# Order of the value products, pace of the feed and bank of the v products in a streaming Conformer step

## The chip, the cores and the metric

The kernel runs on one core of a Trainium2 chip. The metric is device time in microseconds (us). TensorE (PE) multiplies, with weights loaded beside it (PEld); VectorE (DVE), ScalarE (ACT) and GpSimd (POOL) do the elementwise work; SyncE (SP) issues the DMAs. Matrix products are summed in PSUM, which has eight banks.

## The reference, cut to what matters

Two layers, for a prompt of 4096 rows and a sample of 64 rows with a cache of 128 rows; the model has 1024 columns, 16 heads of 64 in two groups of 8, one K/V head for each group.

```python
# layer 0: gated convolution module -> x
kv = rmsnorm(x, kv_g) @ w_kv                     # shared K and V, 2 heads of 64 each
# layer 1
z = rmsnorm(x, pre_g) @ w_in                     # q and gate, 1024 columns each
q, gate = split(z, 2)
s = q / 8 @ k.T - slope * |q_pos - k_pos|        # a query chunk of 64 sees 3 chunks of keys:
                                                 # two past ones and its own
m = max(s.max(), sink); p = exp(s - m)
o = (p / (p.sum() + exp(sink - m))) @ v          # the value products
y = (o * silu(gate)) @ w_out
x = x + rmsnorm(y, post_g)
```

Outputs are y for both streams, the convolution state and the K/V rows of the last window.

## The kernel before, in words

Each f32 operand is split into a high and a low float16 half, and a product is three matmuls: high by high, high by low, low by high. Layer 0 takes the first 1540 us or so. Then come two stages that the change touches.

**Projections (`proj_qkv`, from about 1560 to 1965 us).** Blocks of 256 rows, sixteen of the prompt and one of the sample. The q product of a block is Strassen's scheme of seven products (`strassen`, L942), with accumulators X and W in the PSUM banks tagged "mm" (three) and Z in those tagged "cv" (two, `ps_cz`). X is added to over four products, with a copy by ACT (P1, U2, U3; L953, in the trace U_q and P_q) between them. The order of jobs is written out: p1, p5, K, p6, p2, p7, V of rows 0 to 127, p4, V of rows 128 to 255, p3; after each job comes one step that prepares the next block (`prep_x1`): norms and transposes through PSUM tiles tagged "tr" (two banks; L1023, L1040, L1044). `v_job` (L1161) sums in a tile psv that is also tagged "tr"; `put_v` reads it with ACT (L1140) and DVE (L1141) and stores it.

**Attention (from about 2006 us to the end).** A unit is 128 queries (i) of a block (b) by one K/V head (kv): four units a block, 66 in all, of which 62 are whole (those of the first rows and of the sample are shorter). A unit goes through:

- `att_scores`: scores in "cv" banks (sc, L1491 and L1492), bias and maximum on DVE (L1495), then `stats`: exponentials on ACT (L1522);
- `att_probs`: scaling on POOL (L1541); transposes on PE (ptr, L1557) of three kinds of 128 keys, 0 (two chunks of the past), 1 (one chunk of the past and one of the present) and 2 (the present ones), each put into a float16 tile pT, high half by ACT (L1565, L1562) and then low half by DVE (L1566, L1563);
- `att_values` (L1570): 20 matmuls (pv, L1591) into one bank tagged "s2", of 128 rows by 64 columns each, in pairs for the two heads of a pair (`s_`). For the first 64 queries (par 0) five pairs: kind 0 by high and low V, kind 1 by V; for the second 64 (par 1) five pairs: kind 2, then kind 1;
- `att_out`: times the gate on DVE (L1604), high half by ACT (L1607), low half by DVE.

Between these steps stands filling work from a queue `fill`: the gate projection of the next block (`gate_jobs`, Strassen again: sx_g, sw_g, sz_g, L935), seven products valued 2.75, and the output products of finished rows (`y_jobs`: psy, L179, L180, L182), two halves valued 5.2 for each 128 rows. `filler` takes jobs while a balance is above zero; each unit adds `per` to it in six shares. `force` issues what is left of a block's gate products when its first unit begins. For the last two blocks `per` is worked out from what is left.

The framework then schedules: it goes through this order with a model of the engines' times, and on each engine places the first instruction in program order among those whose inputs are ready by the model. So the order on an engine isn't the program's, and a tile's buffers are given out among those free. It adds all semaphores. DMAs are issued on SP.

Of the kernel before, what the change touches and what calls it, by code (L numbers as in the profile page):

```python
# [12 lines left out]
F32 = mybir.dt.float32  # L13
# [5 lines left out]
P = 128  # L19
# [36 lines left out]
TAIL_D = 0.5  # L56
TAIL_P = 5.2
EARLY_P = 10.0
PER = 10.0
SHARE = (0.2, 0.1, 0.2, 0.1, 0.2, 0.2)  # L60
G_AT = 2

# [5 lines left out]
def tile_streaming_conformer(  # L68
# [17 lines left out]
    pst = ctx.enter_context(tc.tile_pool(name="ps", bufs=2, space=PSUM))  # L86
# [4 lines left out]
    def ps_cv(shape, name):  # L91
        return pst.tile(shape, F32, tag="cv", name=name, bufs=2)

    def ps_s2(shape, name):
        return pst.tile(shape, F32, tag="s2", name=name, bufs=1)
# [79 lines left out]
    def mm3(out, wts, mov, low_last=False):  # L175
        n = len(wts)
        if low_last:
            for i in range(n):
                nc.tensor.matmul(out, wts[i][0], mov[i][0], start=i == 0, stop=False)  # L179
                nc.tensor.matmul(out, wts[i][0], mov[i][1], start=False, stop=False)  # L180
            for i in range(n):
                nc.tensor.matmul(out, wts[i][1], mov[i][0], start=False, stop=i == n - 1)  # L182
            return
        for i in range(n):
            wh, wl = wts[i]
            mh, ml = mov[i]
            nc.tensor.matmul(out, wh, mh, start=i == 0, stop=False)  # L187
            nc.tensor.matmul(out, wh, ml, start=False, stop=False)  # L188
            nc.tensor.matmul(out, wl, mh, start=False, stop=i == n - 1)  # L189
# [27 lines left out]
    def big(shape, dt, name):  # L217
        return wk.tile(shape, dt, tag="big", name=name, bufs=6)
# [207 lines left out]
    with ExitStack() as ph:  # L426
# [64 lines left out]
        ps = pst.tile([P, 4, P], F32, tag="tr", name="pst_apg")  # L491
# [264 lines left out]
        for b in range(SB):  # L756
# [9 lines left out]
            if b + 1 == SAMP_AT:  # L766
                hTs, l, nm, tr = in_jobs(SB)
# [357 lines left out]
    def proj_qkv(b, ht, pool):  # L1125
        t0, T, _, _, _, samp = bb[b]
# [11 lines left out]
        def put_v(src, n, scale, dst, name):  # L1138
            o = pool.tile([P, 2, P], F16, tag="vo", name=name)
            nc.scalar.activation(o[:n, 0], src, AF.Copy, scale=scale)  # L1140
            nc.vector.scalar_tensor_tensor(  # L1141
                out=o[:n, 1], in0=src, scalar=scale, in1=o[:n, 0], op0=ALU.mult, op1=ALU.subtract
            )
            nc.sync.dma_start(out=dst, in_=o[:n])
# [16 lines left out]
        def v_job(i):  # L1161
            n = min(P, T - i * P)
            last = samp or t0 + i * P + n == SEQ
            ps = pst.tile([P, 2 * P], F32, tag="tr", name=f"psv_{b}_{i}")
            wts = [(hT[0][:, kb, i * P : i * P + n], hT[1][:, kb, i * P : i * P + n]) for kb in range(KB)]
            lo = 0 if last else P
            mv = [(w_kv.at(0, kb, lo, 2 * P - lo), w_kv.at(1, kb, lo, 2 * P - lo)) for kb in range(KB)]
            mm3(ps[:n, lo : 2 * P], wts, mv)
            put_v(ps[:n, P:], n, SX / SP, v_scs[WIN:] if samp else v_scr[t0 + i * P : t0 + i * P + n], f"vo_{b}_{i}")
            if last:  # L1170
                kv = big([P, D], F32, f"kvo_{b}")
                nc.scalar.activation(kv[:n, : 2 * P], ps[:n], AF.Copy, scale=1.0 / SP)
                for c, dst in ((0, ck_s if samp else ck_p), (P, cvv_s if samp else cvv_p)):
                    nc.sync.dma_start(
                        out=dst[0, WIN - n : WIN].rearrange("t k d -> t (k d)"), in_=kv[:n, c : c + P]
                    )
# [21 lines left out]
        if samp:  # L1198

            def q_half(half):  # L1200
                ps = ps_mm([P, KH, CH], f"psqs_{half}")
                samp_half(wq, hT, tT, half, ps)
                put_q(half, 0, ps)

            return [k_job, lambda: v_job(0), lambda: q_half(0), lambda: q_half(1)]
# [7 lines left out]

        q = strassen(wq, hT, tT, tmp, out, f"q{b}")
        return [q[0], q[1], k_job, q[2], q[3], q[4], lambda: v_job(0), q[5], lambda: v_job(1), q[6]]

    hts = {}
# [74 lines left out]
    def gate_jobs(b):  # L1292
        t0, T, _, _, _, samp = bb[b]
        gts = CT.setdefault(b, {})["gts"] = {}
        h, t = HT[b]

        def put(nh, i, src, n):
            if i not in gts:
                gts[i] = quad([P, 2, KH, P], F32, f"gt_{b}_{i}")
            go = gts[i][:, nh, :, :n]  # L1300
            nc.scalar.activation(go, src, AF.Tanh, scale=0.5 / SP)
            nc.vector.scalar_tensor_tensor(out=go, in0=go, scalar=1.0, in1=src, op0=ALU.add, op1=ALU.mult)

        if samp:

            def g_half(half):
                ps = ps_mm([P, KH, CH], f"psgs_{half}")
                samp_half(wg, h, t, half, ps)
                put(half, 0, ps, CH)

            return [(2.8, lambda: g_half(0)), (2.8, lambda: g_half(1))]

        def out(nh, th, ps, add):
            src = ps
            if add is not None:
                src = add if (nh, th) == (1, 1) else ps
                nc.vector.tensor_tensor(out=src, in0=ps, in1=add, op=ALU.add)
            put(nh, th, src, P)

        jobs = [(2.75, fn) for fn in strassen(wg, h, t, tmp, out, f"g{b}")]  # L1320
        if b + 1 < nb:
            jobs.append((0.0, lambda: gate_load(b + 1)))
        return jobs
# [134 lines left out]
    with ExitStack() as ph:  # L1458
# [111 lines left out]
        def att_values(b, i, kv):  # L1570
            u = U[b, i, kv]
            npar, first, samp, nm, pts = (u[z] for z in ("npar", "first", "samp", "nm", "pts"))
            prev = vt.get((b, i - 1)) if (i > 0 or samp) else vt.get((b - 1, 1))
            cur = vt[(b, i)]
            po = ps_s2([P, 4, P], f"pv_{nm}")
            vs = slice(kv * HD, kv * HD + HD)
            for par in range(npar):
                mms = []
                full = (0, prev) if par == 0 else (2, cur)
                if full[0] in pts:  # L1580
                    pT, v = pts[full[0]], full[1]
                    for ph_, vh in ((0, 0), (1, 0), (0, 1)):
                        mms.append((v[:, 0, vh, vs], pT[:, ph_]))
                if par == 0 or not first:
                    v = cur if par == 0 else prev
                    for vh in range(2):
                        mms.append((v[:, 1 + par, vh, vs], pts[1][:, par]))
                for q_, (w, m) in enumerate(mms):
                    for s_ in range(2):
                        sl = slice(s_ * 64, s_ * 64 + 64)  # L1590
                        nc.tensor.matmul(po[sl, :, par * CH : par * CH + CH], w, m[:, :, sl], start=q_ == 0, stop=q_ == len(mms) - 1)  # L1591
            u["po"] = po
# [96 lines left out]
        for k, (b, i, kv) in enumerate(units):  # L1689
# [3 lines left out]
            if ui == 0 and b + 1 < nb:  # L1693
                load_att(b + 1)
                fill.extend((c, (b + 1, "g"), fn) for c, fn in gate_jobs(b + 1))
            per = PER
            if b >= nb - 2:
# [17 lines left out]
            while sc:  # L1715
                sc.popleft()()
            att_values(b, i, kv)
            if stats is not None:
                stats()
# [46 lines left out]
```

## Time and profile before

| | us |
|---|---|
| median of 3 runs (2954.96 to 2958.47) | 2955.04 |
| the profiled execution, in all | 2958.04 |
| its span | 2956.3 |
| PE busy | 2803.8 (95%) |
| PEld busy | 1788.6 (61%) |
| DVE busy | 2322.2 (79%) |
| ACT busy | 1885.9 (64%) |
| POOL busy | 1833.2 (62%) |

Shares are means over stages with different limits: up to about 1300 us DVE and POOL are busy nine tenths of the time beside PE, afterwards PE stands alone. A row of PE's instructions in order of time has the start, the time from the first start to the last end, the line, and how many like instructions follow one another; matmuls overlap, so starts tell more than lengths. In brackets stands how long the engine was idle before, and what ended it.

### The profile page before, as it was taken

The numbers are of one execution on the slowest core, as the hardware profiler recorded it, in microseconds if no ns is written. First come the engines' busy times: TensorE is split into PE (matmuls) and PEld (weight loads), VectorE is DVE, ScalarE is ACT, GpSimd is POOL, SyncE is SP. The second block draws the span as 40 slices with busy tenths as digits, with TensorE's granted clock in tenths as the row PEclk, the third lists the DMA queues.
The fourth block names the chain that finished last, engine by engine and source line by source line (L and its number), as shares of the span: only waits on it lengthen the run. The fifth ranks groups of instructions, "written<-read, shape, count | busy, mean of one in ns | idle before, by whom it ended". The sixth has DMA issues, their size and how long they took to land. (4 is left out here: it accounts for less than half of the span.)

```text
span 2956.3 us, 63971 instructions
## 1 busy us (share of the span) xinstructions
PE 2803.8 (95%) x24441; PEld 1788.6 (61%) x24441; DVE 2322.2 (79%) x4373; ACT 1885.9 (64%) x4405; POOL 1833.2 (62%) x1967
## 2 busy tenths in 40 slices
PE   8989999999999988989998999998999999999998
PEld 5444444444444443444458999996777777767774
DVE  6999899999999999988885777745666666656665
ACT  6787776877777675556665777635555555555554
POOL 8899899998898999977742344323333333333332
PEclk9999999999999999999999999999999999999999
DMA  5311211211100125566656666673234223323321
GB/s 183 111 46 41 74 51 43 65 51 47 47 36 33 51 81 169 162 195 196 189 165 192 212 217 229 209 241 118 91 105 125 93 94 122 106 93 98 115 73 48
DMA packets 260601, 341.30 MB, mean 115 GB/s; under 512 B 40549, under 2 KB 184677, under 8 KB 259525
## 3 DMA queue, kind: packets, MB, share of 16 engines
q1 hardware_dynamic: 260293, 337.20, 35.7%
q8 instruction: 192, 3.15, 0.5%
q14 instruction: 116, 0.95, 0.1%
HBM read 206.46 MB, written 130.72 MB: 114 GB/s over the span
## 5 line engine op out<-in xcount | busy, mean ns | idle before, releaser
L597 POOL TENSOR_TENSOR pacc<-pacc,pr 128x512 f32<-128x512 f32 x704 | 908.2, 1306 | 65.6 <-ACT pr L588 38.5
L611 DVE SCALAR_TENSOR_TENSOR acc<-u,pt,acc 128x512 f32<-128x512 f32 x1088 | 789.3, 750 | 17.8
L588 ACT ACTIVATE pr<-u,pt 128x512 f32<-128x512 f32 x704 | 485.6, 716 | 164.2 <-POOL pacc L597 152.2
L1522 ACT ACTIVATE p<-p,st 128x192 f32<-128x192 f32 (+1 forms) x520 | 227.9, 440 | 76.6 <-DVE st L1516 76.3
L1495 DVE CUSTOM_DVE_ANT_0 p<-sc,bias 128x192 f32<-128x192 f32 (+1 forms) x520 | 160.4, 349 | 90.3 <-PE sc L1492 76.0
L1541 POOL TENSOR_TENSOR p<-p,st 128x768 f32<-128x768 f32 (+2 forms) x130 | 186.6, 1456 | 40.9 <-DVE st L1537 26.9
L187 PE MATMUL ps_a<-hT,w_a 128*128 128x512 f16 (+1 forms) x528 | 197.3, 374 | 6.9 <-ACT sg L680 5.4
L187 PE MATMUL ps_gl<-hT,w_gl 128*128 128x512 f16 (+1 forms) x528 | 198.7, 376 | 3.5 <-ACT sig L751 1.9
L188 PE MATMUL ps_gl<-hT,w_gl 128*128 128x512 f16 (+1 forms) x528 | 198.4, 376 | 0.9 <-DVE hT L206 0.9
L187 PE MATMUL ps_gt<-hT,w_gt 128*128 128x512 f16 x512 | 195.8, 382 | 2.8 <-ACT sig L751 2.8
L189 PE MATMUL ps_gl<-hT,w_gl 128*128 128x512 f16 (+1 forms) x528 | 198.4, 376 | 0.0
L179 PE MATMUL psy<-w_oa,hl 128*128 128x512 f16 x512 | 197.3, 386 | 1.0 <-DVE c L611 1.0
L179 PE MATMUL psy<-w_ob,ogT 128*128 128x512 f16 x512 | 194.9, 381 | 3.1 <-ACT ogT L1607 3.1
L180 PE MATMUL psy<-w_oa,hl 128*128 128x512 f16 x512 | 197.5, 386 | 0.0
L188 PE MATMUL ps_a<-hT,w_a 128*128 128x512 f16 (+1 forms) x528 | 197.4, 374 | 0.0
L189 PE MATMUL ps_a<-hT,w_a 128*128 128x512 f16 (+1 forms) x528 | 197.3, 374 | 0.0
L189 PE MATMUL ps_gt<-hT,w_gt 128*128 128x512 f16 x512 | 195.7, 382 | 0.0
L188 PE MATMUL ps_gt<-hT,w_gt 128*128 128x512 f16 x512 | 195.7, 382 | 0.0
L180 PE MATMUL psy<-w_ob,ogT 128*128 128x512 f16 x512 | 195.0, 381 | 0.0
L935 PEld LDWEIGHTS <-w_gS 128*128 128x128 f16 x3072 | 178.4, 98 | 22.7 <-issue 17.6
L935 PEld LDWEIGHTS <-w_qS 128*128 128x128 f16 x3072 | 178.6, 99 | 3.2 <-issue 2.6
L1371 POOL COPY qs<-qraw 128x512 f16<-128x512 f16 (+1 forms) x132 | 75.1, 614 | 136.7 <-PE sc L1492 76.5
(360 smaller groups left out, 7045.7 us busy)
## 6 DMA issues: line engine op xcount, KB each, us to landing
x<-in_x_prompt SPq DMA_DIRECT2D x32, 512.0 KB, 3.7
g_scr<-sg SPq DMA_DIRECT2D x64, 256.0 KB, 2.4
c_scr<-c SPq DMA_DIRECT2D x64, 256.0 KB, 2.0
c<-c_scr SPq DMA_DIRECT2D x32, 512.0 KB, 4.7
g<-g_scr SPq DMA_DIRECT2D x32, 512.0 KB, 4.8
x<-x_scr SPq DMA_DIRECT2D x128, 128.0 KB, 3.6
h_scr<-hTb SPq DMA_DIRECT2D x32, 512.0 KB, 3.7
h_scr<-tTb SPq DMA_DIRECT2D x32, 512.0 KB, 3.6
```

The lines of the kernel that those rows point to most:

```text
L179: nc.tensor.matmul(out, wts[i][0], mov[i][0], start=i == 0, stop=False)
L180: nc.tensor.matmul(out, wts[i][0], mov[i][1], start=False, stop=False)
L187: nc.tensor.matmul(out, wh, mh, start=i == 0, stop=False)
L188: nc.tensor.matmul(out, wh, ml, start=False, stop=False)
L189: nc.tensor.matmul(out, wl, mh, start=False, stop=i == n - 1)
L588: nc.scalar.activation(dst[:, :T], u[:, k : k + T], AF.Identity, scale=wdw[:, j, k : k + 1], bias=pt[:, j, R_DWB : R_DWB + 1] if k == 0 el ...
L597: nc.gpsimd.tensor_tensor(out=pacc[:, :T], in0=pacc[:, :T], in1=dst[:, :T], op=ALU.add)
L611: nc.vector.scalar_tensor_tensor(out=dst[:, :T], in0=u[:, k : k + T], scalar=wdw[:, j, k : k + 1], in1=src[:, :T], op0=ALU.mult, op1=ALU.add,)
L935: nc.tensor.matmul(ps[:, j, :], w[:, wz, kb, j * P : j * P + P], rhs(rz, kb), start=first and j + kb + wz + rz == 0, stop=last and j == KH ...
L1495: nc.vector.tensor_tensor_reduce(out=pbuf[:, t, par * 192 + lo : par * 192 + 192], in0=ps[:, tt, :nk], in1=bias[:, lo:], scale=1.0, scalar ...
L1522: nc.scalar.activation(pp, pp, AF.Exp, scale=2.0 ** -(kv * 4 + t) / SQ, bias=st[:, 1, par, t : t + 1], accum_out=st[:, 3, par, t : t + 1],)
L1541: nc.gpsimd.tensor_tensor(out=pp, in0=pp, in1=st[:, 4, par, :, None].to_broadcast([P, 4, 3 * CH - lo]), op=ALU.mult)
```

## The change

In three places. `att_values` goes through the two halves of the queries the other way round, par 1 first, and for the two full kinds takes the low half of pT before the high half. PER, what a unit adds to the balance of the filling queue, goes from 10.0 to 9.7. And psv, the sum of the v products, is taken from the "cv" banks, where Z and later the scores are, instead of the "tr" banks.

```diff
-PER = 10.0
+PER = 9.7
...
         def v_job(i):
             n = min(P, T - i * P)
             last = samp or t0 + i * P + n == SEQ
-            ps = pst.tile([P, 2 * P], F32, tag="tr", name=f"psv_{b}_{i}")
+            ps = ps_cv([P, 2 * P], f"psv_{b}_{i}")
...
             po = ps_s2([P, 4, P], f"pv_{nm}")
             vs = slice(kv * HD, kv * HD + HD)
-            for par in range(npar):
+            for par in reversed(range(npar)):
                 mms = []
                 full = (0, prev) if par == 0 else (2, cur)
                 if full[0] in pts:
                     pT, v = pts[full[0]], full[1]
-                    for ph_, vh in ((0, 0), (1, 0), (0, 1)):
+                    for ph_, vh in ((1, 0), (0, 0), (0, 1)):
                         mms.append((v[:, 0, vh, vs], pT[:, ph_]))
```

## The prediction

> **What bounds the kernel now.** I read the page first, then the table of stages, then TensorE's instructions in order of time, then the table of waits. The span is 2956.3 us, and the profiled execution took 2958.04 us in all, 3.0 us above the median of the three runs (2955.04 us). The sum below is made against the 2958.04 us and then moved down by those 3.0 us.
>
> ```profile
> span 2956.3 us, 63971 instructions
> ...
> 1700.00:1950.00 250.00, 239.32 (x4070) 233.87 (x4068) 174.85 (x352) 174.99 (x492) 90.79 (x78) 1.00 0.64 210
> 2100.00:2300.00 200.00, 198.21 (x2103) 143.47 (x2101) 125.89 (x389) 112.09 (x367) 72.01 (x120) 1.00 0.35 111
> ...
> 2364.00:2422.00 58.00, 57.80 (x625) 42.22 (x623) 37.03 (x114) 32.51 (x103) 20.46 (x34) 1.00 0.33 106
> 2644.20:2703.50 59.30, 57.86 (x624) 42.26 (x624) 36.97 (x114) 32.14 (x104) 20.50 (x34) 1.00 0.33 104
> ```
>
> The table of stages has busy us of PE, weight loads, DVE, ACT and POOL, then granted clock, DMA share and GB/s. The change touches two stages: the projections (some 1560 to 1965 us) and attention (2006 us to the end). In attention PE is busy 198.21 of 200 us; DVE, the next engine, has 125.89. So PE's own work sets the pace there, and what is taken from it is taken from the time. The last two rows are one attention block each (four units of 128 queries by one KV head): the early kind takes 58.0 us, the late kind 59.3, with the same busy time.
>
> Busy time doesn't tell whether PE streams or stumbles; the start times do. One unit, on PE, in order of time:
>
> ```profile
> 2403.61 0.89 PE L935 MATMUL sx_g<-hl,w_gA 128*128 128x128 f16 x13
> 2404.43 0.30 PE L1591 MATMUL pv<-pT,v_(6, 0)_29279 128*64 128x256 f16 x2
> 2404.66 0.56 PE L935 MATMUL sx_g<-hl,w_gA 128*128 128x128 f16 x7
> ...
> 2405.60 0.41 PE L1591 MATMUL pv<-pT,v_(6, 0)_29279 128*64 128x256 f16 x4
> ...
> 2406.77 0.41 PE L1591 MATMUL pv<-pT,v_(6, 1)_29285 128*64 128x256 f16 x4
> ...
> 2408.66 0.30 PE L1591 MATMUL pv<-pT,v_(6, 1)_29285 128*64 128x256 f16 x2
> ...
> 2409.33 0.41 PE L1591 MATMUL pv<-pT,v_(6, 1)_29285 128*64 128x256 f16 x4
> 2409.57 0.39 PE L1591 MATMUL pv<-pT,v_(6, 0)_29279 128*64 128x256 f16 x4
> 2409.89 0.26 PE L1491 MATMUL sc<-ks,qs 128*128 128x192 f16 x1
> ...
> 2411.13 2.06 PE L935 MATMUL sx_g<-tl,w_gS 128*128 128x128 f16 x34
> 2413.03 0.38 PE L179 MATMUL psy<-w_ob,ogT 128*128 128x512 f16 x1
> ```
>
> The order is not the program's: each part of the value products (pv) is put in as soon as its input is ready, between gate products of other work (sx_g). The 20 pv matmuls of this unit stand in five runs (2, 4, 4, 2, 8).
>
> **What a run costs.** The 34 sx_g take 2413.03 - 2411.13 = 1.90 us, 56 ns each. The 13 before the first run should then end at 2403.61 + 0.73 = 2404.34; pv starts at 2404.43: 0.09 us to get in. Another unit has all its 20 in one run:
>
> ```profile
> 2079.33 1.22 PE L935 MATMUL sx_g<-tl,w_gS 128*128 128x128 f16 x19
> 2080.48 0.52 PE L1591 MATMUL pv<-pT,v_(0, 1)_23834 128*64 128x256 f16 x6
> 2080.83 0.71 PE L1591 MATMUL pv<-pT,v_(1, 0)_24763 128*64 128x256 f16 x10
> 2081.38 0.39 PE L1591 MATMUL pv<-pT,v_(0, 1)_23834 128*64 128x256 f16 x4
> 2081.70 1.51 PE L935 MATMUL sw_g<-hl,w_gA 128*128 128x128 f16 x24
> ```
>
> Two halves of 64 columns run side by side, so 20 matmuls are ten pairs; from 2080.83 to 2081.38 are five pairs, 0.11 us each. Ten take 1.10 of the 1.22 us from 2080.48 to 2081.70: 0.12 us to get out. A run so costs 0.09 + 0.12 = 0.21 us, however long it is. It is paid where the matmuls' shape changes between 128*64 and 128*128.
>
> Over attention I count 203 runs off the same view, from the first to the last:
>
> ```profile
> 2006.32 0.74 PE L1591 MATMUL pv<-pT,v_(0, 0)_23828 128*64 128x256 f16 x10
> ...
> 2943.76 0.38 PE L1591 MATMUL pv<-pT,v_(16, 0)_38519 128*64 128x256 f16 x2
> ```
>
> 195 of them are in the 62 units with 20 matmuls; in these, cuts stand before the 3rd matmul 22 times, the 7th 15, the 11th 37, the 13th 51 and the 17th 8. That is 203 x 0.21 = 43 us of changing over, on the engine that sets the pace.
>
> **Part 1: the order of the value products.** The change adds and removes no instruction here. It puts the second 64 queries (par 1) first, and in them the low half of the last transposed part. That half is the last thing DVE makes for the unit:
>
> ```profile
> 2407.76 0.69 DVE L1566 TENSOR_TENSOR pT<-ptr,pT 128x512 f16<-128x512 f32 x1
> ...
> 2410.66 0.70 DVE L1604 SCALAR_TENSOR_TENSOR pv<-pv,gt 128x512 f32<-128x512 f32 x1
> ```
>
> It ends at 2408.45; its first reader now is the first pair of the unit's last run, at 2409.33, 0.9 us later. If the rest of the products may not overtake, all 20 are ready at once and go as one run. Whether they may not: both par halves write one PSUM bank, in different columns. A case of two outputs in one bank is in the scores:
>
> ```profile
> 2383.05 0.25 PE L1492 MATMUL sc<-ks,qs 128*128 128x192 f16 x1
> ...
> 2383.65 0.25 PE L1492 MATMUL sc<-ks,qs 128*128 128x192 f16 x1
> ...
> 2383.94 0.36 DVE L1495 CUSTOM_DVE_ANT_0 p<-sc,bias 128x192 f32<-128x192 f32 x1 [2.10 <-PE sc L1492]
> ```
>
> DVE had been idle 2.10 us, and its first output was done at 2383.30; still it starts at 2383.94, when the other output of the bank (2383.65 + 0.25 = 2383.90) is done. Work on one bank is kept in program order even where columns differ. I take it that par 0 can't overtake par 1.
>
> Runs after: one per unit, and cuts by other work with precedence. Before, once everything was ready (13th to 20th matmul), such a cut came in 8 units of 62; for 20 instead of 8 matmuls 2.5 times as many, 20. So 62 + 20 = 82 runs instead of 195: 113 x 0.21 = **23.7 us less**. The bounds: 62 runs, 133 x 0.21 = 27.9 less; and below, rival 1.
>
> What covers the later start: the unit's output (L1604) waits for the last product. The one run would start at 2409.33 or sooner and end 1.2 us later, at 2410.5, against 2409.89 before, 0.6 us later; here L1604 starts only at 2410.66 and loses nothing. Elsewhere DVE already waits for pv:
>
> ```profile
> DVE pv L1604 <- PE pv L1591: 40.8, 38, 4.7
> ...
> PE pv L1591 <- ACT pT L1565: 2.7, 4, 1.7
> ```
>
> (us in total, times, longest.) DVE has 37% idle, so a longer wait there costs it nothing; behind it are ACT's copy and the output product, for which PE has other work queued. PE itself has waited 2.7 us for pT in all attention. Cost taken: 0; the end on the other side is rival 3.
>
> **Part 2: PER 10 to 9.7.** No instruction is added; the place of filling work (gate and output products) in program order moves. A block supplies 7 x 2.75 + 4 x 5.2 = 40.05; four units took 40.0 and now take 38.8. Working the queue's arithmetic through, the fill left after a unit falls to 5.2 in early blocks now and to 10.4 in late ones; it would stay at 10.4 or more from the second block on and at 15.6 or more from the sixth, and three gate products (8.3 in all) would be issued by force at starts of late blocks. Loads of the next block's gate inputs on SP follow the last gate product and so move later by up to one unit, behind which 10.4 of output products still stand; SP issues as many as before. The trace prices this by its two kinds of block: idle 0.20 us of 58.0 and 1.44 of 59.3. If every early block became the late kind, 7 x 1.24 = 8.7 us more; if all six late ones became the early kind, 7.4 us less. The new pattern is neither, so I take 0, with both ends kept.
>
> **Part 3: psv into the bank pair of Z and scores.** Z is the second Strassen accumulator (sz_q). In the projections the v product waited for DVE's transposes to give back a "tr" bank:
>
> ```profile
> PE psv L187 <- DVE x L1044: 14.3, 8, 8.9
> ...
> 1563.37 0.58 DVE L1337 TENSOR_SCALAR nsk<-sk 128x1 f32<-128x1 f32 x8 [11.38 <-DMA sk<-in_b_sinks]
> 1564.70 0.29 PE L187 MATMUL psv<-w_kv,hTb 128*128 128x128 f16 x1 [8.87 <-DVE x L1044]
> 1565.20 0.58 ACT L953 COPY U_q<-sx_q 128x512 f32<-128x512 f32 x1
> ...
> 1775.29 0.23 PE L187 MATMUL psv<-w_kv,hTb 128*128 128x128 f16 x1 [0.87 <-DVE x L1044]
> 1777.05 0.58 ACT L953 COPY U_q<-sx_q 128x512 f32<-128x512 f32 x1
> 1777.68 0.72 PE L935 MATMUL sx_q<-tTb,w_qA 128*128 128x128 f16 x10 [0.37 <-ACT U_q L953]
> 1780.36 0.22 PE L187 MATMUL psv<-w_kv,hTb 128*128 128x128 f16 x1
> 1781.50 0.28 DVE L1141 SCALAR_TENSOR_TENSOR vo<-psv,vo 128x128 f16<-128x128 f32 x1
> ```
>
> That wait of 14.3 us goes. What is late next: the product behind v waits for ACT's U copy, which isn't moved. At 1777.68 v would be done 0.87 us sooner and sx_q would still start at 1777.68. The one long wait (8.87 us) comes from DVE standing behind a load of the sinks; U is copied only at 1565.20, so PE waits on. Gain taken 0; at most the 14.3. The cost: Z holds one of the two "cv" banks, so a block's second v product needs the first one's bank, free at 1781.78; it started at 1780.36. That is 1.42 us late, unless PE does Z's last 48 products (2.7 us at 56 ns) first, which nothing here holds back. Cost taken 0, at most rival 2.
>
> **Sum.** 2958.0 - 23.7 + 0 + 0 = 2934.3; less 3.0 for the median: **2931 us**, 0.8% faster.
>
> **Rivals.**
> 1. Par 0 overtakes (columns apart count as free). Then the cuts before the 3rd and the 13th matmul go (low and high halves wait together), those before the 7th, 11th and 17th stay, and the 11th becomes as frequent as the 13th was, 51: 62 + 15 + 51 + 16 = 144 runs, 51 x 0.21 = 10.7 less: 2944 us. For it: scores show DVE against PE, not PE against PE. Chance 0.15.
> 2. The "cv" banks stall PE in the projections: the second v product waits 1.42 us per block, its own bank comes free as much later (1787.5 instead of 1786.1), and the next block's Z, due about 1786.6, waits 0.9: 2.3 x 15 blocks = 35 us, so 2931 + 35 = 2966 us, slower. It decides from 24 / 15 = 1.6 us per block. Against it: Z's last products can go first. PE is busy 239.32 of 250 there, so there is little slack to hide it in. Chance 0.07.
> 3. The saved changes turn into waits: 0.6 us later output in 62 units is 37 us; if two thirds of it came through because PE is short of other work, the 24 us are gone: 2955. Against: PE idles 1.79 of 200 us. Chance 0.08. The Trainium skill, Perfetto Trace Analysis, "Identifying the Most-Contended Engine", speaks for this rival: it says that matmul busy time is no good measure of headroom and that weight-load busy time is. By that rule the stage is at 143.47 of 200 us, 72%, and nothing need be gained. The start times of the trace (56 ns, row after row) disagree, and I go by them.
> 4. The feed also heals the late blocks: 7.4 less, 2924 us. Chance 0.12.
>
> My own case has 0.58. Faster by over 0.2% (5.9 us, about what a measurement of this kernel can tell from no change): 0.58 + 0.15 + 0.12 = 0.85; within 0.2%: 0.08; slower: 0.07. The range: below, 27.9 and 7.4 less, and some of the 14.3 that I took as nothing, 2917; above, rival 1 with part of the feed's 8.7, 2950. Outside lie rivals 2 and 3.
>
> **What would show it.** Right: pv on PE in runs of 20, 70 to 100 runs in all, blocks of 56 to 58 us, and PE busy time in attention lower with as little idle time. psv's wait for DVE gone from the table of waits and sx_q's wait for U_q larger by about as much. Wrong: runs of 6 and 10 (rival 1); PE's psv or sz_q waiting for vo L1141 (rival 2); psy waiting for ogT or pv for pT far above 2.7 us (rival 3); blocks at 59 us and idle sx_g waits (the feed).

## The result and the profile after

The changed kernel takes 2937.04 us (median of 6 runs, 2935.51 to 2940.13), the kernel before, beside it, 2955.0 us: a ratio of 0.9941 [0.9928, 0.9954]. So it is 18 us, 0.6%, faster. The profiled execution took 2936.48 us in all.

The page of the changed kernel first, then its table by stretches (busy us of PE, weight loads, DVE, ACT and POOL, with the number of instructions, then clock, DMA share and GB/s):

```profile
span 2934.5 us, 63935 instructions
...
PE 2774.2 (95%) x24441; PEld 1795.8 (61%) x24441; DVE 2336.9 (80%) x4373; ACT 1883.6 (64%) x4405; POOL 1844.1 (63%) x1967
```

```profile
1700.00:1950.00 250.00, 234.38 (x3928) 230.02 (x3928) 174.84 (x346) 171.25 (x487) 88.29 (x76) 0.99 0.63 206
2100.00:2300.00 200.00, 196.22 (x2171) 149.58 (x2170) 136.40 (x407) 113.00 (x365) 74.53 (x124) 1.00 0.37 116
2100.00:2850.00 750.00, 740.17 (x8247) 565.00 (x8247) 504.12 (x1510) 429.60 (x1384) 280.04 (x454) 1.00 0.34 106
```

The last row has this counterpart in the kernel before:

```profile
2100.00:2850.00 750.00, 738.41 (x7964) 539.98 (x7962) 474.85 (x1444) 411.59 (x1322) 262.05 (x437) 1.00 0.33 104
```

PE's share is 95% in both. The counts are what differs: in the same 750 us of attention PE does 8247 matmuls where it did 7964, and DVE, ACT and POOL do more too. Each of the larger kinds of matmul grew by 3 to 5%, so it is not a shift to shorter ones. In the projections (1700 to 1950 us) it is the other way: 3928 matmuls instead of 4070, with 15.6 us of idle time instead of 10.7. The change gained in one stage and lost in the other.

Unit 27, whose 20 value products stood in five runs, on PE in order of time:

```profile
2401.36 0.38 PE L179 MATMUL psy<-w_ob,ogT 128*128 128x512 f16 x1
2401.67 0.52 PE L1591 MATMUL pv<-pT,v_(6, 1)_29285 128*64 128x256 f16 x6
2402.03 0.71 PE L1591 MATMUL pv<-pT,v_(6, 0)_29279 128*64 128x256 f16 x10
2402.57 0.39 PE L1591 MATMUL pv<-pT,v_(6, 1)_29285 128*64 128x256 f16 x4
2402.89 0.26 PE L1491 MATMUL sc<-ks,qs 128*128 128x192 f16 x1
```

They are one run now. The first six read the V rows of the unit's own block, as par 1 does. The run still costs what was read off before: 2402.89 - 2401.67 = 1.22 us for ten pairs of 0.11 us.

The waits, first of attention and then of the projections (us in total, times, longest):

```profile
DVE pv L1604 <- PE pv L1591: 44.0, 32, 6.3
...
PEld L1591 <- issue: 9.9, 34, 1.0
...
PE ptr L1557 <- DVE pT L1566: 7.6, 3, 3.8
...
PE psy L179 <- ACT ogT L1607: 3.5, 3, 2.4
PE ptr L1557 <- POOL p L1541: 3.1, 3, 2.1
...
PE pv L1591 <- DVE pT L1566: 1.2, 2, 1.0
```

```profile
PE psv L187 <- DVE vo L1141: 17.1, 13, 2.6
PE sx_q L935 <- ACT U_q L953: 10.3, 3, 9.5
```

In attention the waits have changed places. The transposes wait for DVE's pT, which frees their bank, where before they waited for POOL:

```profile
PE ptr L1557 <- POOL p L1541: 8.8, 12, 2.2
...
PE ptr L1557 <- DVE pT L1566: 0.3, 1, 0.3
```

In all, PE's idle time from the first value product to the end is much the same: 31.0 of 918.4 us after, 31.8 of 950.0 before. In the projections the wait for DVE's transposes (14.3 us) is gone, and one of 17.1 us for vo stands in its place. One such place:

```profile
1777.99 0.27 ACT L1140 ACTIVATE vo<-psv 128x128 f16<-128x128 f32 x1
1778.09 2.84 PE L935 MATMUL sx_q<-tTb,w_qA 128*128 128x128 f16 x48
...
1782.31 0.28 DVE L1141 SCALAR_TENSOR_TENSOR vo<-psv,vo 128x128 f16<-128x128 f32 x1
1782.64 0.22 PE L187 MATMUL psv<-w_kv,hTb 128*128 128x128 f16 x1 [1.71 <-DVE vo L1141]
```

ACT reads the first v product at 1777.99, DVE only at 1782.31. Until then the bank isn't free, and the second v product stands on PE 1.71 us. The prediction had 1.42 us for this wait, and named a psv that waits for vo L1141 as a sign of its rival 2.

### The profile page after: what moved, and what is told of

Read it like the earlier page. It is cut to its first block, busy times and chain, and to the rows that moved or that the text cites. A ratio compares the mean times of both kernels' runs of the same rounds, so it can differ in the third digit from the quotient of the medians.

```text
span 2934.5 us, 63935 instructions
## 1 busy us (share of the span) xinstructions
PE 2774.2 (95%) x24441; PEld 1795.8 (61%) x24441; DVE 2336.9 (80%) x4373; ACT 1883.6 (64%) x4405; POOL 1844.1 (63%) x1967
## 5 line engine op out<-in xcount | busy, mean ns | idle before, releaser
L1541 POOL TENSOR_TENSOR p<-p,st 128x768 f32<-128x768 f32 (+2 forms) x130 | 193.1, 1506 | 41.0 <-DVE st L1537 39.7
L1526 POOL TENSOR_TENSOR st<-st 128x8 f32<-128x8 f32 (+1 forms) x66 | 14.4, 218 | 244.1 <-ACT p L1522 134.9
```

The source lines that it names most:

```text
L1541: nc.gpsimd.tensor_tensor(out=pp, in0=pp, in1=st[:, 4, par, :, None].to_broadcast([P, 4, 3 * CH - lo]), op=ALU.mult)
```

## Experiments

Each ratio is against the kernel before on the same chip. Its median there is 2954.85 us for the order alone, PER alone, the bank alone, and order with PER; 2955.22 us for par alone, PER 9.9, PER 9.4, and the second v product last; 2955.8 us for the low half alone, the "mm" banks, P1 on DVE, and the last. "Runs" are counted in the trace as before. A trace is of one execution, so that differences of a few us between two traces can be chance. "Order" is these two edits together:

```diff
-            for par in range(npar):
+            for par in reversed(range(npar)):
...
-                    for ph_, vh in ((0, 0), (1, 0), (0, 1)):
+                    for ph_, vh in ((1, 0), (0, 0), (0, 1)):
```

**The order alone** (both edits above; PER 10, psv in "tr").

> The new order of the value products alone; PER stays 10.0 and psv stays in the tr banks. In the program's own order of PE instructions the value products stand in 70 runs (200 before, 80 in the whole change). Theory A (each run costs 0.21 us of changing shape, and nothing else matters): 130 x 0.21 = 27 us less than before, some 2928 us, below the whole change. Theory B (the slower feed made much of the gain): 10 to 14 us less, some 2943 us. Theory C (the v bank made part of it): 15 to 20 us less.

Measured: 2943.35 us, 0.9962 [0.9951, 0.9973], 73 runs. 130 fewer runs at 0.21 us should have given 27 us (theory A); 11.5 came, which is the size that theory B named. The trace is of the slowest of the six executions (2950.45 us, 7 above the median), so its idle time is on the high side. Its table of waits in attention, and below it the one row of the kernel before:

```profile
DVE pv L1604 <- PE pv L1591: 63.7, 43, 6.3
PE sx_g L935 <- ACT P_g L953: 15.6, 11, 1.7
...
PE sc L1491 <- DVE mx L1495: 7.4, 16, 1.1
PE psy L179 <- ACT ogT L1607: 3.9, 5, 2.0
```

```profile
PE sx_g L935 <- ACT P_g L953: 2.6, 11, 0.4
```

The 13 us more of the wait for P_g are nearly as much as what is missing. Where it sits, on PE and on ACT:

```profile
2404.86 1.78 PE L935 MATMUL sx_g<-hl,w_gA 128*128 128x128 f16 x29
...
2407.96 0.25 PE L1492 MATMUL sc<-ks,qs 128*128 128x192 f16 x1
2409.57 1.39 PE L935 MATMUL sx_g<-tl,w_gS 128*128 128x128 f16 x22 [1.37 <-ACT P_g L953]
...
2411.61 0.52 PE L1591 MATMUL pv<-pT,v_(6, 1)_29285 128*64 128x256 f16 x6
```

```profile
2407.80 0.44 ACT L1522 ACTIVATE p<-p,st 128x192 f32<-128x192 f32 x1
...
2408.35 0.59 ACT L1565 CAST pT<-ptr 128x512 f16<-128x512 f32 x1
2408.95 0.58 ACT L953 COPY P_g<-sx_g 128x512 f32<-128x512 f32 x1
```

PE has finished a gate product at about 2406.6 and can't begin the next before ACT, busy with exponentials and a cast, has copied its sum. At this very place the kernel before had value products to do (2408.66, 2409.33 and 2409.57 in the prediction's rows). Now they come at 2411.61, when PE is busy anyway. In this place the cut pieces had been filling work.

**PER 9.7 alone.**

```diff
-PER = 10.0
+PER = 9.7
```

> PER 9.7 alone. The program's order has 247 runs of value products, 47 more than before. Theory A: 47 x 0.21 = 10 us more, some 2965 us. Theory B: 7 to 10 us less. Theory C: no change.

Measured: 2947.79 us, 0.9975 [0.9964, 0.9986], 250 runs: 7 us faster, as theory B had it, although it has 47 more runs, some 10 us of changing. Its row of the same 750 us:

```profile
2100.00:2850.00 750.00, 748.48 (x8008) 537.82 (x8005) 489.63 (x1476) 421.37 (x1354) 272.20 (x449) 1.00 0.35 106
```

PE idles 1.5 us there, against 11.6 before: with the slower feed it always has something queued.

**The v products in "cv" alone.**

```diff
-            ps = pst.tile([P, 2 * P], F32, tag="tr", name=f"psv_{b}_{i}")
+            ps = ps_cv([P, 2 * P], f"psv_{b}_{i}")
```

> psv in the cv banks alone. 199 runs, as before. Theory A: the wait for DVE's transposes (14.3 us) gives way to waits for vo (L1141) and U_q, and the time stays within 5 us of before. Theory C: 5 to 10 us less. If the cv banks cost time: 5 to 10 us more, and PE's waits in the projections some 5 us longer than before, as in the whole change.

Measured: 2963.99 us, 1.0032 [1.002, 1.0044]: 9.1 us slower, the last case of the expectation. PE's waits in its projections:

```profile
PE psv L187 <- DVE vo L1141: 17.0, 13, 2.6
PE sx_q L935 <- ACT U_q L953: 9.8, 2, 9.5
```

Against the rows before (14.3 for psv, and 4.2 for U_q in the row below) that is 17.0 + 9.8 - 14.3 - 4.2 = 8.3 us more, near the 9.1 us lost. It is not all there is to the stage, though. Other waits got shorter (PE's tot for ACT's hTb from 4.0 to 1.0 us, and 2.7 us of sx_g for a DMA are gone), and PE's idle time from 1540 to 1985 us rises by 3.9 us, from 25.9 to 29.8. So the rows name the wait, and the trace shows less than half of the loss as idle time there.

```profile
PE sx_q L935 <- ACT U_q L953: 4.2, 8, 1.6
```

**Order and PER 9.7** (the whole change with psv left in "tr"). The edits are the first two diffs.

> The whole change without the v bank: new order and PER 9.7, psv in the tr banks. 83 runs. Theory A: 117 x 0.21 = 25 us less than before, some 2930 us; if the cv banks cost 5 us in the whole change, this is that much faster than it. Theory C: some 5 to 10 us slower than the whole change. Against the order alone it shows what the slower feed does once the runs are whole: A says 13 x 0.21 = 3 us more, B says 5 or more less.

Measured: 2924.77 us, 0.9898 [0.9885, 0.9911], 86 runs. That is 30 us below before, while the two parts alone gave 11.5 and 7.1. Theory B had 5 us or more for the slower feed on top of the order; it is 18.6. The same 750 us, first of the order alone, then of this kernel:

```profile
2100.00:2850.00 750.00, 729.18 (x8127) 559.50 (x8125) 478.72 (x1470) 417.96 (x1339) 268.40 (x446) 1.00 0.34 105
```

```profile
2100.00:2850.00 750.00, 740.85 (x8283) 566.73 (x8281) 506.73 (x1519) 429.99 (x1386) 280.72 (x459) 1.00 0.35 107
```

Idle time falls from 20.8 to 9.2 us, matmuls rise from 8127 to 8283, and no row of sx_g waiting for P_g is left in its table. Against the whole change it is also the test of the bank in place: 0.9898 against 0.9941, 12 us. The first value product marks the start of attention, in the changed kernel and in this one:

```profile
2016.07 0.74 PE L1591 MATMUL pv<-pT,v_(0, 0)_23828 128*64 128x256 f16 x10
```

```profile
2003.82 0.74 PE L1591 MATMUL pv<-pT,v_(0, 0)_23828 128*64 128x256 f16 x10
```

It comes 12.2 us later in the changed kernel, and the two spans differ by 9.9 us. That does not show, however, that the whole difference is there before attention begins. From these starts to the end PE does 9721 matmuls in the changed kernel and 9828 in this one. So 107 more, nearly all of them gate products, stand ahead of the mark, some 6 us at 56 ns each. The last product of the projections ends between 1977.7 and 1985.4 us in the nine kernels with psv in "tr" (1978.5 in this one, 1985.6 in the changed one), so two traces can't settle 7 us. PE's idle time from 1540 to 1985 us is 24.1 us here and 30.8 in the changed kernel, about half of the 12 us. What the bank costs, and through which wait, is shown by the two experiments that take the wait away (the second v product last, and the "mm" banks).

**Par 1 first, without the low half's change; and the low half first, without par's.** Each is one of the two edits of the order, at PER 10.

```diff
-            for par in range(npar):
+            for par in reversed(range(npar)):
```

> Half of the order alone: the second 64 queries first, but high before low half of pT as before; PER 10.0, psv in tr. 127 runs of value products in the program's order: a pair, then 18. Theory A (0.21 us for each run): 57 runs more than the order alone, 12 us slower than it, and 73 x 0.21 = 15 us faster than before by the runs alone. Theory D (what the order saves comes back as a wait of sx_g for P_g once a block, because the value products no longer stand between): the wait is there as with the order alone (15.6 us in all), so about no faster than before, 2952 to 2957 us.

```diff
-                    for ph_, vh in ((0, 0), (1, 0), (0, 1)):
+                    for ph_, vh in ((1, 0), (0, 0), (0, 1)):
```

> Low before high half of pT, the first 64 queries still first; PER 10.0, psv in tr. 142 runs in the program's order. By runs alone 58 x 0.21 = 12 us less than before, 2943 us; by theory D some of it comes back as waits of sx_g for P_g, between 2.6 us (before) and 15.6 us (order alone): 2944 to 2954 us.

Measured: 2947.57 us, 0.9974 [0.9965, 0.9983], 130 runs, and 2942.14 us, 0.9953 [0.994, 0.9965], 143 runs. The wait for P_g in each:

```profile
PE sx_g L935 <- ACT P_g L953: 6.7, 10, 0.7
...
PE pv L1591 <- ACT pT L1565: 4.6, 8, 0.8
```

```profile
PE sx_g L935 <- ACT P_g L953: 5.6, 7, 1.7
```

Theory D's times were missed in both: the first was to be 2952 to 2957 us with the whole wait for P_g, and has 6.7 of the 15.6 us; the second came out below 2944, where the runs alone had put it (2943). The second is as fast as the whole order with twice its runs. At PER 10 the count of runs does not tell the time.

It does tell how long PE is busy. From the first value product to the end, the kernels with psv in "tr" do the same matmuls. Busy and idle time of PE in that stretch (us, one execution each):

| psv in "tr" | runs | busy | idle |
|---|---|---|---|
| PER 9.7 alone | 250 | 924.8 | 18.7 |
| before | 203 | 918.2 | 31.8 |
| low half first, alone | 143 | 903.1 | 32.3 |
| par 1 first, alone | 130 | 903.4 | 38.2 |
| order, PER 9.4 | 86 | 890.5 | 28.0 |
| order, PER 9.7 | 86 | 890.8 | 30.0 |
| order, PER 9.9 | 83 | 892.7 | 32.8 |
| order, PER 10 | 73 | 895.9 | 44.6 |
| order, PER 10, P1 on DVE | 71 | 897.1 | 38.2 |

From 250 to 86 runs, both at PER 9.7, busy time falls by 34.0 us, 0.21 us for each run, and idle time rises by 11.3. At PER 10, from 203 to 73 runs, busy time falls by 22.3, 0.17 each, and idle time rises by 12.8. So the price of a run holds roughly; most of what is missing in the times is idle time of PE, and at one PER there is more of it the fewer the pieces are. (The rows with PER 9.4 and 9.9 and with P1 on DVE belong to experiments further down.)

**The pace, with the order** (PER 9.9 and 9.4; psv in "tr").

```diff
-PER = 10.0
+PER = 9.9
```

> New order, psv in tr, PER 9.9 (10.0 gave 2943, 9.7 gave 2925). 80 runs. Theory D: any pace below the supply (40.05 a block against 4 x 9.9 = 39.6) builds up a backlog in time, slower than 9.7 does: the wait for P_g stays in the early blocks and goes in the late ones, 2928 to 2936 us. If the gain is in the runs alone: 2941 us or more.

```diff
-PER = 10.0
+PER = 9.4
```

> New order, psv in tr, PER 9.4. 83 runs. Theory D: the backlog comes sooner, more gate products are issued by force, and the wait for P_g stays gone: 2921 to 2930 us, as with 9.7. If the even pace itself counts and not the backlog, the force undoes it: 2932 us or more.

Measured: 2933.95 us, 0.9923 [0.991, 0.9937], 83 runs, and 2923.46 us, 0.9891 [0.9875, 0.9906], 86 runs. With the order, PER 10, 9.9, 9.7 and 9.4 give 0.9962, 0.9923, 0.9898 and 0.9891: the first tenth brings more than half, and from 9.7 on nothing that the intervals tell apart. At 9.9 PE waits for P_g three times, 2.2 us in all, at 2123.5, 2180.5 and 2238.1 us, in early blocks, and not after that, as theory D expected of a backlog that builds up.

**The second v product last** (the whole change, and p3 of the q product ahead of V of rows 128 to 255).

```diff
-        return [... lambda: v_job(0), q[5], lambda: v_job(1), q[6]]
+        return [... lambda: v_job(0), q[5], q[6], lambda: v_job(1)]
```

> The whole change, with the second v product moved behind Z's last product (p3) in the job list of the projections. 81 runs. If the v bank costs its 9 to 12 us through that product's wait for the first one's bank (PE psv <- DVE vo L1141, 17.1 us), the wait goes and the time falls to that of the version without the v bank, 2925 to 2929 us. If it costs through something else (the banks shared with Z and the first scores), it stays at 2935 us or more.

Measured: 2920.61 us, 0.9888 [0.9872, 0.9903]. PE's waits in the projections have no psv row any more:

```profile
PE sx_q L935 <- ACT U_q L953: 11.2, 2, 9.5
PE sz_q L935 <- DVE q L1187: 8.8, 9, 1.1
```

The next block's Z waits for a bank instead, 8.8 us in all. That is about half, and with it the 12 us of the bank are back, and perhaps 4 more (the intervals overlap with those of order and PER 9.7); the time is a little below the 2925 to 2929 us expected. The two waits differ by 8.3 us and the two times by 16.4, so the rows do not account for all of it.

**The v products in "mm"** (order, PER 9.7).

```diff
-            ps = pst.tile([P, 2 * P], F32, tag="tr", name=f"psv_{b}_{i}")
+            ps = ps_mm([P, 2 * P], f"psv_{b}_{i}")
```

> New order, PER 9.7, psv in the three mm banks (X and W stand in two of them). 81 runs. If the release of a shared bank is what costs, W is free before the second v product and nothing waits: 2918 to 2926 us, no slower than with tr (2925). If any bank shared with Strassen's accumulators costs as the cv banks did: 2932 us or more.

Measured: 2922.66 us, 0.9889 [0.9876, 0.9903]. Three banks instead of two:

```profile
PE psv L187 <- DVE q L1187: 4.9, 8, 1.3
```

The wait is 4.9 instead of 17.1 us. So it was the pair of "cv" banks, not the leaving of "tr", that cost the time.

**The gate's copy P1 on DVE** (with the order, at PER 10): the wait that seemed to have taken the order's gain is taken away.

```diff
-            nc.scalar.copy(X[name], src)
+            (nc.vector.tensor_copy if name == "P1" and nm[0] == "g" else nc.scalar.copy)(X[name], src)
```

> The new order alone (PER 10.0, psv in tr), with one more edit: the copy of the first gate product (P_g, L953) on DVE instead of ACT, where it stood behind eight exponentials. 68 runs. Theory D (with the order alone the saved time comes back as sx_g's wait for P_g, 15.6 us): the wait goes and the time falls from 2943 to 2928 to 2934 us, without a slower feed. If that wait is only where PE's lack of other work shows, another wait of the same 15 us takes its place: 2940 us or more.

Measured: 2941.87 us, 0.9957 [0.9944, 0.9971], against 0.9962 without it. Waits and stretch:

```profile
PE sc L1491 <- DVE mx L1495: 11.2, 12, 1.6
PE ptr L1557 <- DVE pT L1566: 6.7, 7, 2.4
...
PE sx_g L935 <- DVE P_g L953: 0.8, 1, 0.8
```

```profile
2100.00:2850.00 750.00, 735.69 (x8143) 564.14 (x8142) 505.23 (x1490) 412.08 (x1335) 268.47 (x446) 0.99 0.34 106
```

The wait for P_g falls from 15.6 to 0.8 us, and the time stays. PE waits longer for scores' banks and for transposes' (11.2 and 6.7 us, where the order alone had 7.4 and 3.6): some 7 of the 15 us are seen again there. So that copy by itself was not what held the time; it was one of the places where PE ran out of other work. This is a miss for the reading that the first experiment's rows suggest.

**The best of it together** (the whole change, second v product last, PER 9.4).

```diff
-PER = 10.0
+PER = 9.4
...
-        return [... lambda: v_job(0), q[5], lambda: v_job(1), q[6]]
+        return [... lambda: v_job(0), q[5], q[6], lambda: v_job(1)]
```

> The whole change with the second v product last in the projections' jobs, and PER 9.4. 84 runs. 9.4 was as good as 9.7 with psv in tr (2923 against 2925), so 2917 to 2923 us, as with 9.7 (2921).

Measured: 2915.54 us (2914.43 to 2916.26), 0.9865 [0.9852, 0.9879], 87 runs: 40 us below the kernel before, a little under the expected 2917 to 2923, and the fastest of all.

```profile
2100.00:2850.00 750.00, 745.20 (x8249) 566.08 (x8247) 501.65 (x1530) 430.76 (x1388) 278.90 (x457) 1.00 0.34 106
```

## Why the prediction was right, and where it was not

2937 us lies in the range of 2917 to 2950, on the side that was forecast; the likeliest value, 2931, was 6 us too low. That the sum came so near is luck. Its three terms were off by 12.2 us (the order gave less), 18.6 us (PER gave more) and 12.3 us (the bank cost), and these nearly cancel.

- **Where PE was the bound, and what a run costs: right.** The price stands in the rows after as before (1.22 us for ten pairs). In the Trainium skill, TensorEngine Tiling (Array Packing), "Key Properties", a change of tiling mode is said to drain TensorE, with no price. The trace agrees in that each change costs time, 0.09 us in and 0.12 us out; that a drain is what takes it, no run here shows. Over attention the saving came in full: from before to after PE's busy time there falls from 918.2 to 887.4 us, some 6 of it for the 107 matmuls that moved ahead of the first value product, which leaves 25 us for 120 runs, 0.21 each.
- **The number of runs: right.** 82 were forecast for the 62 whole units; there are 75 (49 units in one run, 12 in two of 6 and 14, one in two of 1 and 19), and 83 in all attention. Cuts by other work came in 13 units, not 20.
- **Par 0 doesn't overtake (rival 1 refuted).** The runs are of 20, or of 6 and 14, not of 6 and 10 beside others. Par 0 did have the occasion: in unit 27 of the changed kernel DVE ends the last input of par 0 (the first L1563) at 2395.17 and the last of the unit (L1566) at 2398.90, 3.7 us later. Rival 1's own sum has 16 cuts before the 17th matmul where the prediction counts 8, and gives no reason; with 8 it is 136 runs, not 144.
- **The step "Cost taken: 0" for the later start of the products failed.** The order by itself gave 11.5 us, not 23.7. The output did come later: with the order alone DVE waits 63.7 us for pv instead of 40.8. But PE's wait for ogT, through which that would reach it, is 3.9 us (3.1 in the kernel before), so it is not the late output of rival 3 that cost it. What cost it is rival 3's condition, "PE is short of other work": the pieces of value products had stood in holes, and without them the holes showed (20.8 us idle in 750 instead of 11.6, and 14.3 with P1 on DVE, whose traced execution is 1.4 us under its median). The argument against rival 3, that PE idles 1.79 of 200 us, failed twice: it was read off a good stretch (31.8 of 950.0 us over all of attention), and it was circular, as PE idled so little because the pieces were there.
- **The step "so I take 0" for PER failed.** It was bounded by idle time of two kinds of block that exist in the trace before (-7.4 to +8.7 us). By itself it gave 7.1 us, as rival 4 had it; with the order it gave 18.6 (2943.35 to 2924.77), well outside those bounds. The bounds were for PER with the old order. What PER does, work in reserve when a chain is late, is worth more once the pieces are gone. The two parts had to be costed together.
- **The step "Cost taken 0" for psv's bank failed.** The prediction had the place and nearly the size of the wait (1.42 us forecast, 1.71 us there), and dismissed it because Z's last products could go first. They did not: the second v product stands ahead of them on PE, and PE waits; with p3 put ahead of it by hand the wait is gone. It came 13 times, 17.1 us in all. Of the 14.3 us that went, some 6 came back as a longer wait for U_q (4.2 to 10.3 us, as forecast, nearly all at the first block). So the first half of rival 2 came true. Its second half, the next block's Z waiting for a bank, did not (Z's one wait, 0.9 us, is for its input tTb), and the loss, 9 us alone and 12 in the whole, is far from its 35.
- **The sum, as measured:** -11.5 for the order, -18.6 for PER with it, +12.3 for the bank, together -17.8 us, against -23.7, 0 and 0. The first two steps are from one chip, the last compares two batches of runs by their medians; by the intervals, some 5 us of each of the last two are uncertain.

Open: that more filling work is the common cause is inferred from the four values of PER, from where the wait for P_g stands at 9.9, and from the copy that changed nothing; the queue's content at each wait was not measured. What fixes how much idle time each order and each PER leaves is not shown either. The low half's edit alone, with 143 runs, is as fast as both edits with 73 because PE idles 12.3 us less (32.3 against 44.6, the latter in an execution 7 us over its median) against 7.3 us more of busy time, but no run says why just that much. And about half of what the bank costs stands in no row of waits shown here.

## What to carry to other kernels

A piece of work that looks badly placed on the busiest engine may be standing in a hole: before merging such pieces, ask what that engine will do in those moments instead, and cost the merger together with whatever keeps other work in reserve. Judge a stage on a saturated engine by the instructions that it gets through in a fixed stretch, as here PE's busy time hardly moved (738 to 740 of 750 us) while the count rose by 3.6%. Putting a tile into another pair of banks is a change of order: look up when its last reader comes (here DVE, 4.3 us behind ACT) and which product needs that bank next, and move that product or take the larger pool.

## What was not expected of the hardware

Nothing in the engines' durations. What was new is the cost of changing between 128*64 and 128*128 matmuls as a term of its own: 0.21 us for each run, 43 of 950 us of attention before the change; between the two kernels at PER 9.7 the busy time shows the same price, 34.0 us for 164 runs.
